# Two groups of stores on ScalarE's queue, an earlier bias strip, and two pinned silus in a two-layer kernel

## The chip, the cores and the metric

The kernel runs on one core of one Trainium2 chip, as one program. The metric is the device time of that program in microseconds, the median of several runs. Five engines work side by side, each through its own instructions in a fixed order: TensorE (PE; its weight loads are listed as PEld), VectorE (DVE), ScalarE (ACT), GpSimd (POOL) and SyncE (SP). An engine that meets an instruction whose inputs are not ready stands still, and so does all that is queued behind it. Transfers between the core's memory and DRAM are issued by an engine as an instruction and then run on 16 DMA engines.

## The reference, cut to what matters

Two blocks on x of 1024 positions by 1024 features, float32. The first is a gated delta rule beside a stick-breaking attention. The second is this:

```python
z = rms_norm(x) @ w_in
y_mla  = mla_group(z)     # q, k by two small projections, rms norm, rope; 8 heads, block-causal softmax
y_diff = diff_group(z)    # 4 heads, two maps each: softmax(q k + bias[bucket(k - q)]), a0 - lam * a1
x = x + concat(y_mla, y_diff) @ w_out
h = rms_norm(x)
g = causal_conv3(h @ w_gate) + conv_b
x = x + (silu(g) * (h @ w_up)) @ w_down
x = x + sigmoid(rms_norm(x) @ w_ple_gate) * (p @ w_ple_proj)
```

## The kernel before

A float32 factor is kept as a rounded high half and the remainder as a low half, and a product takes three matmuls (`mm3`: high by high, high by low, low by high). Weights come from DRAM as a `raw` tile and are split into an `hl` pair (`W`, with POOL doing both halves, L255 and L256). A scheduler puts the instructions of all engines in an order from priorities; code in a `high_priority` block is moved ahead of what was written before it, and `keep_in_program_order` holds an instruction behind all that its engine was given before. Every transfer of this kernel is issued by SP.

**Staged projections.** `qk_stack` (queries and keys of the stick-breaking attention in layer 1, of the diff attention in layer 2) and `mla_proj` (the latent attention) compute rows by position, normalize them, transpose them on PE (L768, L1151) into a PSUM tile, and split that tile into a staging tile: ACT casts the high half (L313), DVE subtracts for the low half (L314; both lines are in the helper `split_evac`). The staging tile goes to DRAM: 32 tiles `qb_st` from L771 (16 in each layer, into `dr_qk` and `dr_dqk`) and 32 tiles `l_st` from L1154 (into `dr_mla`, 384 KB each). There are three `l_st` buffers, and two `qb_st` buffers in layer 1 but one in layer 2. In the same stretch ACT squares the PSUM results (`qb_sq` L750, `l_sq` L1103 and L1125), DVE multiplies by gains, sums the squares and takes the inverse root (L291 to L306), and POOL scales by it.

**Start of the diff attention.** It comes after the latent attention, interleaved with `ple_proj` (the product of p with `w_pp`, whose results `p_o` go to DRAM as `dr_pp`, L1454 and L1455, two buffers). For each head, `first` loads a bias `strip` (512 KB, L1309), and POOL fills a corner of it (L1311). DVE then adds the strip to the logits `z` of a block and takes the row maximum (L1341, L1342), ACT takes the exponential (L1344), and PE transposes (L1364) and multiplies by the values (L1367). The weight `lam` of the second map is loaded at L1284 and worked out on DVE and ACT (L1286 to L1293). `ahead` runs before, within the latent attention, and loads the first head's queries and keys.

**The feed-forward product.** `ffn` has 11 groups of 256 hidden features. A group is two calls of `wino`, one for the gate and one for the up product, each seven products of 128x512 with twelve matmuls. The seven, in PE's order, are B11 into accumulator x, B21 into z, T2 onto x, T1 into y, T3 onto x, T4 into q and B22 onto y. Between them ACT copies x out three times (`w_u`, L1571; below u1, u2 and u3): T2 may not start before u1 is out, nor T3 before u2. `out` adds an accumulator and a copy: in the up product that is `f_c` (DVE, L1621), followed by `f_y` = `f_y` times `f_c` (DVE, L1622), for the four quarters (0,0) with u1, (1,1) with u3, (1,0) and (0,1). B22 may not start before `f_c` of (1,1) has read y. `f_y` holds the convolution of the gate product (DVE, L1612 and L1614), and the silu (ACT, L1616) is applied to it in place, in two halves: ct 1 first, then ct 0, the half that `f_y` of (0,0) needs.

Of the kernel before, what the change touches and what calls it, by code (L numbers as in the profile page):

```python
# [11 lines left out]
F32 = mybir.dt.float32  # L12
# [152 lines left out]
class Kern:  # L165
# [572 lines left out]
    def qk_stack(self, pool, xn, ws, gains, dst):  # L738
# [23 lines left out]
        def stack(gi, half, raw):  # L762
            for pr in range(2):
# [7 lines left out]
                nc.sync.dma_start(dst[p, :, a:a + 2, half * 512:half * 512 + 512], st.bitcast(F32))  # L771
# [277 lines left out]
    def mla_proj(self):  # L1049
# [96 lines left out]
        def fin(raw, hg, half, part):  # L1146

            for h in range(4):
                pt = self.PT()
                for j in range(4):  # L1150
                    nc.tensor.transpose(pt[:96, j, :], raw[:, j, h, :], self.ident)  # L1151
                st = lp.tile([96, 2, 512], F32R, tag="l_st", name="l_st", bufs=3)
                self.split_evac(st[:, 0], st[:, 1], pt[:96].rearrange("p a b -> p (a b)"))
                nc.sync.dma_start(self.dr_mla[4 * hg + h, 0:96, part:part + 2, half * 512:half * 512 + 512], st.bitcast(F32))  # L1154
# [110 lines left out]
    def ahead(self):  # L1265
# [4 lines left out]
        self.qk0 = self.load_qk(self.qp, self.dr_dqk[0], 0)  # L1270
        yield 0.0

    def diff(self):
# [30 lines left out]
        def first(hd):  # L1304
            qk = [self.load_qk(qp, self.dr_dqk[hd], 0) if hd else self.qk0]
            o = sp.tile([128, NT, 128], F32, tag="o", name="o", bufs=2)
            skew = self.dr_f[hd][0:1, 127:128]
            strip[hd] = sp.tile([128, 1024], F32, tag="strip", name="strip", bufs=2)
            nc.sync.dma_start(strip[hd], bass.AP(tensor=skew.tensor, offset=skew.offset, ap=[[1152, 128], [1, 1024]]))  # L1309

            nc.gpsimd.memset(strip[hd][0:64, 960:1024], NEG)  # L1311
# [125 lines left out]
    def ple_proj(self):  # L1437

        nc, d = self.nc, self.d
        with self.pool("pp") as fp:  # L1440
            pT = [self.pair(fp, f"pT{h}", 2) for h in range(2)]
            for h in range(2):
                for k in range(2):
                    pr = fp.tile([128, 512], F32, tag="p_raw", name="p_raw", bufs=1)
                    nc.sync.dma_start(pr, d["pT"][:, k, h * 512:h * 512 + 512])
                    nc.scalar.copy(pT[h][0][:, k], pr)
                    nc.gpsimd.tensor_tensor(pT[h][1][:, k], pr, pT[h][0][:, k].bitcast(F32), ALU.subtract)
            for gi in range(4):
                w = self.W(d["w_pp"][gi])
                for tp in range(4):  # L1450
                    ps = self.tm(w, pT, 2, tp)
                    for j in range(2):
                        o = fp.tile([128, 256], F32, tag="p_o", name="p_o", bufs=2)
                        nc.scalar.copy(o, ps[:, j])  # L1454
                        nc.sync.dma_start(self.dr_pp[gi, tp, :, j], o)  # L1455
                    yield 0.25
# [135 lines left out]
    def ffn(self):  # L1592

        nc, d, tc, vec = self.nc, self.d, self.tc, self.vec
        with self.pool("ffn", 1) as fp:
            for gi in range(11):
# [19 lines left out]
                silu = lambda y: nc.scalar.activation(y, y, AF.Silu)  # L1616
# [104 lines left out]
```

## Time and profile before

| what | value |
|---|---|
| time, median of 3 runs | 2645.79 us (2638.98 to 2645.89) |
| the profiled execution | 2637.64 us |
| its span, first to last instruction | 2635.9 us |
| mean granted TensorE clock | 0.982 |
| PE busy, share of the span | 2490.2 us, 94% |
| DVE, POOL, ACT busy | 1435.8, 1054.8, 869.3 us (54%, 40%, 33%) |
| DMA engines, mean | 119 GB/s |

Busy time is summed for each engine over the span; the engines overlap. A clock of 1.00 is TensorE's higher level, 2.4 GHz, and 0.50 its lower, 1.2 GHz. The profiled execution lies 1.3 us below the fastest of the three runs and 8.2 us below their median. PE has 146 us of the span in which it does nothing, spread over the stages.

### The profile page before, as it was taken

How to read it: one execution, taken by the hardware profiler on the slowest of the kernel's cores; microseconds unless marked ns; L12 is line 12 of the kernel's file. 1: busy time of each engine (PE TensorE's matmuls, PEld its weight loads, DVE VectorE, ACT ScalarE, POOL GpSimd, SP SyncE). 2: the span in 40 equal slices, each digit the busy share in tenths (PEclk: the TensorE clock that was granted, in tenths of full speed). 3: DMA queues.
4: the chain of work that ended last, by engine and by line, in shares of the span. 5: the costliest groups of instructions: out<-in, count | busy, mean ns of one | idle time of the engine just before them, and what ended most of it. 6: DMA issues, size and time to landing. Idle time of an engine off the chain costs nothing.

```text
span 2635.9 us, 38621 instructions
## 1 busy us (share of the span) xinstructions
PE 2490.2 (94%) x15170; PEld 2119.0 (80%) x15170; DVE 1435.8 (54%) x2677; ACT 869.3 (33%) x1599; POOL 1054.8 (40%) x914
## 2 busy tenths in 40 slices
PE   6999999999999999998899989988999999999999
PEld 6888999876777779988787868887777777777789
DVE  5565555275666553368854338846544544433372
ACT  3322223163444341123334346624333333100030
POOL 1524332122122245544533322224777777533322
PEclk9999999999999999999999999989999999999999
DMA  4433223253422455322675457451222122523222
GB/s 163 141 110 112 81 89 105 65 151 97 116 84 69 167 177 180 115 72 90 203 214 167 120 186 205 136 188 58 67 92 80 64 89 87 185 79 104 72 85 93
DMA packets 158766, 313.55 MB, mean 119 GB/s; under 512 B 14804, under 2 KB 62164, under 8 KB 158456
## 3 DMA queue, kind: packets, MB, share of 16 engines
q1 hardware_dynamic: 158584, 311.07, 37.8%
q8 instruction: 120, 1.97, 0.3%
q14 instruction: 62, 0.51, 0.1%
HBM read 214.01 MB, written 100.42 MB: 119 GB/s over the span
## 4 chain that ended last, share of the span: by engine, by line
PE 40%; DVE 9%; DMA 3%; issue 2%; ACT 2%; POOL 1%; SPq 0%; ACTq 0%; DVEq 0%; POOLq 0%
PE pj L1567 13%; PE pj L266 6%; PE pj L264 6%; PE pj L265 6%; DVE f_y L1614 1%; PE po L932 1%; PE pt L925 1%; PE po L1367 1%; DVE f_y L1612 1%; PE z L1337 1%; PE z L264 1%; DVE rs_a L304 1%; PE z L265 1%; PE z L266 1%; DMA f_y<-dr_h 1%
## 5 line engine op out<-in xcount | busy, mean ns | idle before, releaser
L255 POOL TENSOR_SCALAR hl<-raw 128x512 fp32r<-128x512 f32 (+2 forms) x262 | 192.7, 740 | 897.4 <-PE pj L266 884.1
L256 POOL TENSOR_TENSOR hl<-raw,hl 128x512 fp32r<-128x512 f32 (+3 forms) x270 | 367.7, 1369 | 34.0 <-ACT hl L253 17.9
L265 PE MATMUL pj<-hl,xn_0h 128*128 128x256 f32 (+2 forms) x544 | 159.0, 292 | 2.7 <-POOL hl L256 2.7
L264 PE MATMUL pj<-hl,xn_0h 128*128 128x256 f32 (+2 forms) x544 | 160.4, 295 | 0.6 <-DVE qb_st L314 0.6
L264 PE MATMUL pj<-hl,xn_1h 128*128 128x256 f32 (+2 forms) x544 | 159.6, 293 | 0.0
L266 PE MATMUL pj<-hl,xn_0l 128*128 128x256 f32 (+2 forms) x544 | 159.3, 293 | 0.0
L265 PE MATMUL pj<-hl,xn_1h 128*128 128x256 f32 (+2 forms) x544 | 157.3, 289 | 0.0
L266 PE MATMUL pj<-hl,xn_1l 128*128 128x256 f32 (+2 forms) x544 | 157.2, 289 | 0.0
L1548 POOL TENSOR_TENSOR hl<-w_s,hl 128x512 fp32r<-128x512 f32 x88 | 117.6, 1341 | 66.9 <-ACT hl L1547 66.7
L266 PE MATMUL pj<-hl,f_hl 128*128 128x512 f32 x352 | 139.8, 399 | 2.3 <-DVE f_hl L1653 2.3
L264 PE MATMUL pj<-hl,f_hh 128*128 128x512 f32 x352 | 139.7, 397 | 2.0 <-DVE xres L1662 1.6
L1548 POOL TENSOR_TENSOR hl<-raw,hl 128x512 fp32r<-128x512 f32 x66 | 103.1, 1568 | 91.5 <-ACT hl L1547 91.5
L265 PE MATMUL pj<-hl,f_hh 128*128 128x512 f32 x352 | 138.9, 395 | 0.0
L1662 DVE TENSOR_TENSOR xres<-xres,pj 128x512 f32<-128x512 f32 x96 | 65.2, 686 | 129.9 <-PE pj L266 118.2
L264 PE MATMUL pj<-xn_0h,hl 128*128 128x512 f32 x288 | 117.6, 408 | 0.0
L264 PE MATMUL pj<-xn_1h,hl 128*128 128x512 f32 x288 | 116.6, 405 | 0.0
L927 DVE COPY aT<-pt 128x512 f32<-128x512 f32 (+1 forms) x112 | 70.6, 630 | 83.6 <-PE pt L925 83.4
L265 PE MATMUL pj<-xn_1l,hl 128*128 128x512 f32 x288 | 116.1, 403 | 0.0
L266 PE MATMUL pj<-xn_0h,hl 128*128 128x512 f32 x288 | 115.1, 400 | 0.0
L265 PE MATMUL pj<-xn_0l,hl 128*128 128x512 f32 x288 | 114.8, 398 | 0.0
L266 PE MATMUL pj<-xn_1h,hl 128*128 128x512 f32 x288 | 114.4, 397 | 0.0
L1605 DVE TENSOR_TENSOR f_u<-pj,w_u 128x512 f32<-128x512 f32 x44 | 30.3, 689 | 148.6 <-ACT w_u L1571 96.5
(595 smaller groups left out, 7316.9 us busy)
## 6 DMA issues: line engine op xcount, KB each, us to landing
raw<-in_w_o_dram SPq DMA_DIRECT2D x28, 512.0 KB
qk<-dr_mla SPq DMA_DIRECT2D x32, 416.0 KB
dr_mla<-l_st SPq DMA_DIRECT2D x32, 384.0 KB
raw<-in_w_fg_dram SPq DMA_DIRECT2D x22, 512.0 KB
raw<-in_w_fu_dram SPq DMA_DIRECT2D x22, 512.0 KB
dr_h<-f_y SPq DMA_DIRECT2D x22, 512.0 KB
raw<-in_w_fd_dram SPq DMA_DIRECT2D x22, 512.0 KB
f_y<-dr_h SPq DMA_DIRECT2D x22, 512.0 KB
```

The costliest lines, as they stand in the source:

```text
L255: nc.gpsimd.tensor_scalar(hl[:, 0], raw[:, k:k + c], 1.0, 1.0, ALU.mult, ALU.mult)
L256: nc.gpsimd.tensor_tensor(hl[:, 1], raw[:, k:k + c], hl[:, 0].bitcast(F32), ALU.subtract)
L264: mm(ps, lh[0], rh[0], start=first, stop=False)
L265: mm(ps, lh[0], rh[1], start=False, stop=False)
L266: mm(ps, lh[1], rh[0], start=False, stop=last)
L304: nc.vector.tensor_tensor(a, y, y, ALU.mult)
L925: nc.tensor.transpose(pt[:, b, :], e[a][:, j * 128:j * 128 + 128], self.ident)
L927: copy[j0 // 2 % 2](aT[:, :n], pt[:, :n])
L1548: nc.gpsimd.tensor_tensor(hl[:, 1], v, hl[:, 0].bitcast(F32), ALU.subtract)
L1567: nc.tensor.matmul(ps, w[k][l], b[r][:, k, :], start=first and k + n == 0, stop=k == 3 and n == 2, skip_group_check=not first)
L1605: nc.vector.tensor_tensor(u, ps, v, ALU.add)
L1662: nc.vector.tensor_tensor(xr, xr, ps, ALU.add)
```

## The change

The stores of L771 and L1154 are issued by ACT in place of SP. The first strip is loaded in `ahead` by a new function, and the strips' tile moves from the diff attention's pool to the pool that `ahead` opens. `ple_proj` loads its four weights first and holds one pair of tiles `pT` at a time, one half of the positions after the other, where it held both. The two silus of a feed-forward group are kept in program order, behind the copies u2 and u3 of the up product. The line numbers of the changed kernel are 5 higher from L1310 on.

```diff
@@ qk_stack
-                nc.sync.dma_start(dst[p, :, a:a + 2, half * 512:half * 512 + 512], st.bitcast(F32))
+                nc.scalar.dma_start(dst[p, :, a:a + 2, half * 512:half * 512 + 512], st.bitcast(F32))
@@ mla_proj, fin
-                nc.sync.dma_start(self.dr_mla[4 * hg + h, 0:96, part:part + 2, half * 512:half * 512 + 512], st.bitcast(F32))
+                nc.scalar.dma_start(self.dr_mla[4 * hg + h, 0:96, part:part + 2, half * 512:half * 512 + 512], st.bitcast(F32))
@@ ahead
         self.qk0 = self.load_qk(self.qp, self.dr_dqk[0], 0)
+        self.strip0 = self.load_strip(0)
         yield 0.0
+
+    def load_strip(self, hd):
+        skew = self.dr_f[hd][0:1, 127:128]
+        strip = self.qp.tile([128, 1024], F32, tag="strip", name="strip", bufs=2)
+        self.nc.sync.dma_start(strip, bass.AP(tensor=skew.tensor, offset=skew.offset, ap=[[1152, 128], [1, 1024]]))
+
+        self.nc.gpsimd.memset(strip[0:64, 960:1024], NEG)
+        return strip
@@ diff, first
-            skew = self.dr_f[hd][0:1, 127:128]
-            strip[hd] = sp.tile([128, 1024], F32, tag="strip", name="strip", bufs=2)
-            nc.sync.dma_start(strip[hd], bass.AP(tensor=skew.tensor, offset=skew.offset, ap=[[1152, 128], [1, 1024]]))
-
-            nc.gpsimd.memset(strip[hd][0:64, 960:1024], NEG)
+            strip[hd] = self.load_strip(hd) if hd else self.strip0
@@ ple_proj
-            pT = [self.pair(fp, f"pT{h}", 2) for h in range(2)]
+            ws = [self.W(d["w_pp"][gi]) for gi in range(4)]
             for h in range(2):
+                pT = self.pair(fp, "pT", 2)
                 for k in range(2):
                     pr = fp.tile([128, 512], F32, tag="p_raw", name="p_raw", bufs=1)
                     nc.sync.dma_start(pr, d["pT"][:, k, h * 512:h * 512 + 512])
...
-            for gi in range(4):
-                w = self.W(d["w_pp"][gi])
-                for tp in range(4):
-                    ps = self.tm(w, pT, 2, tp)
...
+                for gi in range(4):
+                    for tp in range(2 * h, 2 * h + 2):
+                        ps = self.tm(ws[gi], [pT, pT], 2, tp)
...
@@ ffn
-                silu = lambda y: nc.scalar.activation(y, y, AF.Silu)
+                silu = lambda y: tc.keep_in_program_order(nc.scalar.activation(y, y, AF.Silu))
```

The scheduler turns this into new orders. The first place is ScalarE in the projections of layer 2, where the tiles `l_st_12000` to `l_st_12027` are staged (numbers tell the buffers apart). Before, SP holds their four stores behind two weight loads of the diff attention's value projection:

```order
L248 DMA raw_13798<-in_w2_dv_dram 128x1024 [waits DMAHW4_49,Pool_49]
L248 DMA raw_13806<-in_w2_dv_dram 128x1024 [waits DMAHW5_49,Pool_49]
L1154 DMA dr_mla_10149<-l_st_12000 96x2x512 [waits DMAHW6_49,DVE_49]
L1154 DMA dr_mla_10149<-l_st_12009 96x2x512 [waits DMAHW7_49,DVE_49]
L1154 DMA dr_mla_10149<-l_st_12018 96x2x512 [waits DMAHW0_49,DVE_49]
```

In the changed kernel the stores stand on ACT, each behind the cast of its high half and some of them behind or ahead of a square:

```order
L313 CAST l_st_12000<-pt_11995 96x512 [waits DMAHW7_49,PE_49]
L313 CAST l_st_12009<-pt_12004 96x512 [waits DMAHW1_49,PE_49]
L1154 DMA dr_mla_10149<-l_st_12000 96x2x512 [waits DVE_49]
L750 ACTIVATE qb_sq_11991<-pj_11942 128x512 [waits PE_49]
L1154 DMA dr_mla_10149<-l_st_12009 96x2x512 [waits DVE_49]
L313 CAST l_st_12018<-pt_12013 96x512 [waits DMAHW2_49,PE_49]
L313 CAST l_st_12027<-pt_12022 96x512 [waits DMAHW4_49,PE_49]
```

The weight loads are no longer ahead of the stores, and each store now waits on ACT for DVE's low half, with the next square or cast queued behind it.

The second place is ScalarE in the feed-forward product, one up product of the middle groups. Before:

```order
L1547 CAST hl_18738<-raw_18734 128x512 [waits DMAHW3_49,PE_49,Activation_49]
L1616 ACTIVATE f_y_18579<-f_y_18579 128x1024 [waits DMAHW4_49,DVE_49]
L1547 CAST hl_18741<-raw_18736 128x512 [waits DMAHW5_49,PE_49,Activation_49]
L1571 COPY w_u1_18635<-pj_18620 128x512
L1616 ACTIVATE f_y_18583<-f_y_18583 128x1024 [waits DMAHW6_49,DVE_49]
```

In the changed kernel:

```order
L1552 CAST hl_18741<-raw_18736 128x512 [waits DMAHW5_49,PE_49,Activation_49]
L1576 COPY w_u1_18635<-pj_18620 128x512 [waits DVE_49]
L1552 CAST hl_18748<-w_s_18746 128x512 [waits PE_49,Activation_49,Pool_49]
L1552 CAST hl_18751<-w_s_18744 128x512 [waits PE_49,Activation_49]
L1576 COPY w_u2_18661<-pj_18620 128x512 [waits DVE_49]
L1621 ACTIVATE f_y_18579<-f_y_18579 128x1024 [waits DMAHW4_49,DVE_49]
L1552 CAST hl_18756<-w_s_18754 128x512 [waits PE_49,Activation_49,Pool_49]
L1552 CAST hl_18759<-raw_18736 128x512 [waits PE_49,Activation_49]
L1576 COPY w_u3_18688<-pj_18620 128x512
L1621 ACTIVATE f_y_18583<-f_y_18583 128x1024 [waits DMAHW6_49,DVE_49]
```

The copy u1 has lost the silu ahead of it, and the silu that `f_y` of (0,0) needs (`f_y_18583`) stands behind u3. DVE's order of `f_c` and `f_y` is as before: (0,0), then (1,1). The third place is TensorE at the end of such an up product, where B22 follows T4. In the changed kernel four matmuls of the next gate product stand between them; before, B22 followed T4 directly and B11 came after it:

```order
L1572 MATMUL pj_18411<-T4h_17985,hl_18326 128x512
L1572 MATMUL pj_18481<-B11h_17389,hl_18452 128x512
L1572 MATMUL pj_18481<-B11l_17390,hl_18452 128x512
L1572 MATMUL pj_18481<-B11h_17389,hl_18452 128x512 x2
L1572 MATMUL pj_18336<-B22h_17983,hl_18331 128x512
```

So B22 starts four matmuls later in PE's row. The last group has no gate product behind it and keeps the old order there.

## Rows read from the trace of the kernel before

**Rows 1.** Busy time by stretch: PE, PEld, DVE, ACT, POOL, clock, DMA share

```profile
1230.00:1250.00 20.00, 16.25 (x105) 15.58 (x104) 20.00 (x43) 6.26 (x13) 12.39 (x10) 0.85 0.43 135
1308.00:1330.00 22.00, 21.95 (x171) 21.64 (x170) 19.23 (x68) 7.82 (x18) 8.56 (x6) 0.90 0.78 246
...
1577.00:1586.00 9.00, 7.76 (x26) 6.33 (x27) 6.19 (x32) 5.41 (x19) 0.00 (x0) 0.53 0.70 264
...
1853.00:1894.00 41.00, 40.23 (x167) 32.42 (x167) 16.88 (x20) 12.95 (x22) 30.59 (x22) 0.96 0.21 70
```

**Rows 2.** Timelines of DVE, SP, ACT and PE around 1300 (start, us, engine, line)

```profile
1293.31 1.87 DVE L314 TENSOR_TENSOR l_st<-pt,l_st 96x512 fp32r<-96x512 f32 x3
...
1297.06 4.03 SPq L248 DMA_DIRECT2D raw<-in_w_dv_dram  x2
1301.18 2.86 SPq L1154 DMA_DIRECT2D dr_mla<-l_st  x3
...
1306.27 0.58 ACT L313 CAST l_st<-pt 96x512 fp32r<-96x512 f32 x1 [7.92 <-DMA dr_mla<-l_st]
...
1307.62 1.09 PE L1151 MATMUL pt<-cst,l_raw 128*96 128x128 f32 x4 [7.45 <-DVE l_st L314]
```

**Rows 3.** Instructions of the staging tile's store (ns: least, median, most)

```profile
L1154 SPq DMA_DIRECT2D dr_mla<-l_st x32: 304/327/1890, 1234.3 to 1338.1; - x32
```

**Rows 4.** Timelines of ACT and DVE: both halves of one staging tile

```profile
1243.56 0.58 ACT L313 CAST l_st<-pt 96x512 fp32r<-96x512 f32 x1 [0.23 <-PE pt L1151]
...
1248.84 0.68 DVE L314 TENSOR_TENSOR l_st<-pt,l_st 96x512 fp32r<-96x512 f32 x1
...
1290.97 0.60 ACT L750 ACTIVATE qb_sq<-pj 128x512 f32<-128x512 f32 x1 [5.78 <-DVE rs_y L306]
```

**Rows 5.** Timelines of SP, ACT, POOL and PE at the diff attention's start

```profile
1569.50 0.35 SPq L1284 DMA_DIRECT2D lam<-in_lam_dram  x1
...
1570.96 0.32 SPq L1309 DMA_DIRECT2D strip<-dr_f  x1
...
1569.90 0.37 ACT L1454 COPY p_o<-pj 128x256 f32<-128x256 f32 x1 [2.98 <-DMA dr_pp<-p_o]
...
1573.92 0.29 DVE L1286 TENSOR_TENSOR lam_p<-lam 128x128 f32<-128x128 f32 x1 [6.48 <-DMA lam<-in_lam_dram]
...
1576.43 0.14 POOL L1311 MEMSET strip<- 64x64 f32 x1 [7.90 <-DMA strip<-dr_f]
...
1576.96 0.47 PE L1337 MATMUL z<-k,q 128*128 128x128 f32 x1 [9.91 <-DVE a_nm L1341]
```

**Rows 6.** PE's waits from 1813 to 2270: total, times, longest

```profile
PE pj L1567 <- ACT w_u L1571: 10.4, 10, 2.0
```

**Rows 7.** Timelines of PE in the first group, of ACT in the second

```profile
1853.77 0.51 PE L1567 MATMUL pj<-T2h,hl 128*128 128x512 f32 x1 [2.02 <-ACT w_u L1571]
...
1893.21 1.06 ACT L1616 ACTIVATE f_y<-f_y 128x1024 f32<-128x1024 f32 x1 [3.72 <-DVE f_y L1614]
```

**Rows 8.** Timelines of PE, ACT, DVE and POOL around T4 of the second group

```profile
1903.75 0.39 PE L1567 MATMUL pj<-T4h,hl 128*128 128x512 f32 x1
...
1906.53 0.40 PE L1567 MATMUL pj<-B22h,hl 128*128 128x512 f32 x1
...
1904.53 0.58 ACT L1571 COPY w_u<-pj 128x512 f32<-128x512 f32 x1
...
1898.59 0.69 DVE L1622 TENSOR_TENSOR f_y<-f_y,f_c 128x512 f32<-128x512 f32 x1 [0.32 <-ACT f_y L1616]
1905.14 0.69 DVE L1621 TENSOR_TENSOR f_c<-pj,w_u 128x512 f32<-128x512 f32 x1 [5.86 <-ACT w_u L1571]
1905.87 1.72 DVE L1622 TENSOR_TENSOR f_y<-f_y,f_c 128x512 f32<-128x512 f32 x1
...
1905.76 1.28 POOL L1553 TENSOR_TENSOR w_s<-w_s,raw 128x512 f32<-128x512 f32 x1
```

**Rows 9.** Timeline of PE at the end of the last group

```profile
2270.19 0.50 PE L1567 MATMUL pj<-B22h,hl 128*128 128x512 f32 x1 [3.28 <-DVE f_c L1621]
```

More of the change, by code (lines that the diff above doesn't have):

```diff
@@ L1445, in ple_proj @@
                     nc.sync.dma_start(pr, d["pT"][:, k, h * 512:h * 512 + 512])
-                    nc.scalar.copy(pT[h][0][:, k], pr)
-                    nc.gpsimd.tensor_tensor(pT[h][1][:, k], pr, pT[h][0][:, k].bitcast(F32), ALU.subtract)
-            for gi in range(4):
-                w = self.W(d["w_pp"][gi])
-                for tp in range(4):
-                    ps = self.tm(w, pT, 2, tp)
[L1452 to L1456, printed above, removed]
+                    nc.scalar.copy(pT[0][:, k], pr)
+                    nc.gpsimd.tensor_tensor(pT[1][:, k], pr, pT[0][:, k].bitcast(F32), ALU.subtract)
+                for gi in range(4):
+                    for tp in range(2 * h, 2 * h + 2):
+                        ps = self.tm(ws[gi], [pT, pT], 2, tp)
+                        for j in range(2):
+                            o = fp.tile([128, 256], F32, tag="p_o", name="p_o", bufs=2)
+                            nc.scalar.copy(o, ps[:, j])
+                            nc.sync.dma_start(self.dr_pp[gi, tp, :, j], o)
+                        yield 0.25
     def mix_late(self):
```

## The prediction

> **What bounds the kernel now.** I read the page first. PE is busy for 2490 of 2636 us, and the change takes no matmul away, so a gain can only come from the 146 us in which PE stands still and from the time in which its clock is at the lower level. I then listed PE's idle stretches with what ended each, and looked at the four places that the change touches.
>
> In the projections of layer 2, PE stands still once for 7.45 us [rows 2]. The chain behind it: the transposes L1151 waited for DVE's low half, that for ACT's cast, and the cast had waited 7.92 us for a staging buffer, which three stores still held. DVE had finished the three low halves at 1293.31 + 1.87 = 1295.2, but SP issued the stores only from 1301.18, because two weight loads stood ahead of them from 1297.06 to 1301.09. So the data were ready 6 us before the stores went. In the 22 us after the stretch the clock is 0.90 [rows 1]: 22 x 0.10 = 2.2 us more. Elsewhere in this stage DVE is full: all 20.00 of 20 us, with PE at 16.25 [rows 1].
>
> At the diff attention's start PE stands still for 9.91 us [rows 5]. The strip was issued at 1570.96 and its corner filled at 1576.43, 5.4 us later; the first maximum and PE's next matmul follow. Then the clock is 0.53 for 9 us [rows 1], its lower level nearly throughout: 9 x 0.47 = 4.2 us.
>
> In the feed-forward product PE waits ten times for a copy `w_u`, 10.4 us [rows 6]: 2.02 us in the first group [rows 7], (10.4 - 2.02) / 9 = 0.93 in nine others. It is u1, held up by a silu of 1.06 us [rows 7] that waits for the convolution. After the first one the clock is 0.96 over 41 us [rows 1], 1.6 us. The last group has another wait, 3.28 us, before B22 [rows 9].
>
> **The stores on ACT.** Taken away: the 7.45 us, with the 2.2 us of clock, 9.7 at most, since the stores would go at 1295.2, while ACT casts its next `l_st` only after 1300. Added: an issue takes 0.33 us (median) [rows 3], and the 48 of layer 2 come to 16 us of an engine that is a third busy. That is cover enough, but for the order. A store waits on ACT for DVE's low half, which can be late: one tile's cast ended at 1244.1 and its low half at 1249.5, 5.4 us after [rows 4]. Squares queue behind the store, DVE sums them, and DVE is full here, so what it waits for is not made good. I price one such hand-over by the square and the issue, 0.60 + 0.33 = 0.9 us [rows 3, 4]. Where the next instruction of DVE does not need that square, it costs nothing. I take 6 hand-overs of the 48, 5.7 us, since the full stretches are only part of the stage and PE is not always behind DVE: 9.7 - 5.7 = **-4 us**. Bounds: -10 with none, +8 with 20 of them. In layer 1 the 16 stores are covered by the same free ACT; 0, bound +5 (16 x 0.33, every issue paid).
>
> A page of the Trainium skill speaks against this part: DMA: Bandwidth & Descriptors, "Issuing engines are not separate DMA queues", says that transfers from all engines run on the same 16 DMA engines and that a second issuing engine saves only the issue time. By that alone this part would bring 0. The row shows another loss than bandwidth, a store behind a waiting load in one engine's order, so I keep -4 and carry the rule as a rival.
>
> **The strip and `ple_proj`.** Taken away: 9.91 + 4.2 = 14.1 us. Late next are three things. `lam` took 1573.92 - 1569.50 = 4.4 us to arrive [rows 5] and its place in the row is hardly earlier; but the first maxima no longer stand behind it, and matmuls of `ple_proj` now lie between the first logits and the transposes. The `p_o` copies wait for their stores, up to 2.98 us [rows 5], and now share ACT with the diff attention's exponentials. And the second pair `pT` can be filled only when the first half's last matmul is done: cast 0.58, subtraction 1.28 (like POOL's in [rows 8]), a load of half the strip's size (estimate 2.7 to 5.4 us from its 5.4), again cast and subtraction, 6.4 to 9.1 us; matmuls of the latent attention cover perhaps 5 of it. I charge 2.5 for the pair and 4.5 for the other two: 14.1 - 7 = **-7 us**. Bounds: -13 with nearly all hidden, 0 when what is late next takes the whole place of the strip.
>
> **The silus.** u1 comes free, so the ten waits go. In their place B22 waits. Before, u3 ended at 1904.53 + 0.58 = 1905.1. Now the silu follows, to 1906.1; then DVE does `f_y` of (0,0), and only after it `f_c` of (1,1), 0.69 us, which B22 needs. `f_y` takes 0.69 us alone but 1.72 us where a POOL operation of 1.28 us has just begun [rows 8]. So y is read at 1906.1 + 0.69 + 0.69 = 1907.5, or at 1908.5. B22 stood at 1906.53 and now has four matmuls more ahead of it, (1906.53 - 1903.75) / 12 = 0.23 each [rows 8]: due at 1907.46. The new wait is about 0.1 or 1.1 us. POOL is busy for 30.6 of 41 us here [rows 1], so I take 0.8.
>
> The rule for this is on the page SBUF — State Buffer, "Who interferes with whom": a DVE instruction with two inputs in SBUF contends with a GpSimd instruction that reads SBUF, and the loser waits for the whole instruction. The trace agrees (1.72 against 0.69); were it so every time, this part would cost 9 x (1.1 - 0.93) = +1.5 in the middle groups, and by the short row it would bring -7.5.
>
> Middle groups: 9 x (0.8 - 0.93) = -1.2. First group: 2.02 + 1.6 goes, 0.8 comes: -2.8. Last group: no gate product follows, and `f_c` of (1,1) stands behind one more `f_y`: +1.0 (0.69 to 1.72). Together **-3 us**, bounds -10 and +1.
>
> **Sum.** 2637.64 - 4 - 7 - 3 = 2623.6. The profiled execution lies 1.3 us below the fastest of the three runs and 8.2 below their median, so the median may come out higher than the sum; I forecast 2625. 0.3% (8 us) is about what a measurement of this kernel can tell from no change.
>
> **Rivals.**
> 1. All three waits go and nothing comes back: -10 - 13 - 10 gives 2605; two of three about 2612. For it: the data stood ready 6 us before the stores, and nothing but the strip held DVE at 1576. Against it: DVE is full in the one stage, and the second `pT` has a chain of its own. Chance 0.17.
> 2. What is late next takes the place: the strip's 14 us go to the second `pT` and the `p_o` stores, and the silus to B22. 2637.64 - 4 + 0 + 1 = 2635. For it: ACT already waits for `p_o` stores. Chance 0.17. The case of the first page's rule, the stores bring 0 and the rest is as forecast, gives 2628; chance 0.08, and lies within the forecast's range.
> 3. The feed-forward wait is moved and PE's clock falls after it, as after the 2.02 us: 10 x 1.6 = 16 us on top of the forecast, 2641. Against it: after the nine waits of 0.93 us the middle groups keep their pace; for it: the new wait may reach 1.1 and more. Chance 0.08.
> 4. Slower: ACT, held by stores that wait for DVE, holds DVE in turn. If all 48 hand-overs are paid, 48 x 0.9 = 43 us against 9.7: 2637.64 + 33 - 10 = 2661. It decides from 31 hand-overs on (31 x 0.9 = 28, the 9.7 + 7 + 3 of the gains and 8 us more). For it: DVE is full and low halves come up to 5.4 us late. Against it: ACT is a third busy and works ahead. Chance 0.08.
>
> **How the numbers follow.** The forecast has 0.42; its own range is 2615 to 2635, from the three terms' bounds taken one at a time. The first rival reaches down to 2605 and the second and third up to 2641; 2608 to 2644 leaves out some 2 in 10. Faster by over 0.3%, below 2637.9 against the median shown: nearly all of the forecast and rival 1, the page's case, and about half of rival 2, which after the 8 us between profile and median lies at the edge: 0.66. Slower: rival 4 and a little of 3: 0.09. The rest, 0.25, is the same.
>
> **What would show it.** Right: no idle stretch of PE above 2 us at 1300 and no cast waiting 7.92 us for a store; the first maximum at once after the latent attention's last matmul; `w_u` gone from PE's waits, and `f_c` L1626 there about ten times at 0.1 to 1.1 us. Wrong: ACT waiting long at its stores while DVE idles before L752 or L1105; PE waiting for `pTl` or for `p_o` copies; a clock below 0.95 in the middle groups. The forecast fails most easily at the 6 hand-overs, which no row counts, and at the 7 us charged at the diff attention's start.

## Result and the profile after

The changed kernel takes 2626.43 us (median of 4 runs, 2625.82 to 2628.09), the kernel before 2644.97 (4 runs, 2638.98 to 2645.89). The ratio is 0.9936, with a 95% interval from 0.9921 to 0.9952: faster by 0.6%, more than the 0.3% that a measurement can tell from no change. The profiled execution takes 2626.64 us, 11.0 less than that of before; the medians differ by 18.5, because the profile of before lay below its runs.

The page of the changed kernel, its span and its busy times:

```profile
span 2624.8 us, 38588 instructions
...
PE 2488.8 (95%) x15170; PEld 2118.0 (81%) x15170; DVE 1435.2 (55%) x2677; ACT 866.9 (33%) x1599; POOL 1074.6 (41%) x914
```

PE does the same work in 11 us less span. Where they came from is read from PE's rows that open a stage: the first transpose `pt<-cst,n_xs` of layer 2, the first transpose of the latent projections (L1091), the first logits `z` of the latent attention, the last matmul on a `mix` tile, the first feed-forward product. The differences of their start times, in us:

| stage | before | changed | difference | predicted |
|---|---|---|---|---|
| layer 1 | 1071.3 | 1068.9 | -2.4 | 0 |
| projections, from L1091 to the latent attention | 155.4 | 161.9 | **+6.5** | -4 |
| latent and diff attention, to the last `mix` matmul | 450.2 | 442.6 | **-7.6** | -7 |
| feed-forward product to the end | 807.1 | 799.7 | **-7.4** | -3 |

The row that parts the second line of this table from the third, the first logits of the latent attention, does not stand at the same place in PE's work. Of the 480 matmuls `pj<-hl,xn_0h` and `pj<-hl,xn_0l` between L1091 and the last `mix` matmul, 359 stand ahead of it before and 384 in the changed kernel. They follow each other at 0.12 us, so 25 x 0.12 = 3.0 us of the +6.5, and as much of the -7.6, are work that moved from one line to the other. At equal work the two lines read +3.5 and -4.6; their sum is not touched.

**Projections.** The 7.45 us in which PE stood still [rows 2] are gone from their place, and the stage is longer. The whole stage, before and in the changed kernel (PE, PEld, DVE, ACT, POOL, clock, DMA share):

```profile
1194.30:1349.66 155.36, 134.51 (x986) 128.45 (x983) 128.15 (x340) 52.09 (x111) 74.71 (x60) 0.95 0.56 176
```

```profile
1191.60:1353.46 161.86, 140.92 (x1011) 134.10 (x1009) 124.82 (x340) 51.75 (x111) 74.81 (x60) 0.94 0.55 169
```

PE does nothing for 155.36 - 134.51 = 20.85 us before and for 161.86 - 140.92 = 20.94 now: the idle time of the stage did not fall at all. Of the +6.5, 3.0 are the moved matmuls and some 1.6 the clock (0.94 in place of 0.95); the rest is not put down to anything here. PE's waits now (line, what was waited for, total, times, longest):

```profile
PE pt L1151 <- POOL l_raw L1110: 5.4, 2, 3.2
PE pt L1151 <- DVE l_st L314: 4.8, 3, 3.0
PE pt L768 <- DVE l_st L314: 3.4, 1, 3.4
PE pt L768 <- POOL qb_raw L759: 2.4, 1, 2.4
PE pt L1151 <- DVE qb_st L314: 2.1, 1, 2.1
```

One long gap has become several shorter ones, most of them waits for a scaled row of POOL or a low half of DVE. In the busiest 50 us DVE is no longer full. Before, and in the changed kernel:

```profile
1250.00:1300.00 50.00, 47.30 (x331) 43.63 (x330) 46.86 (x130) 20.17 (x49) 25.63 (x21) 0.96 0.62 199
```

```profile
1250.00:1300.00 50.00, 43.15 (x291) 39.37 (x290) 40.55 (x117) 18.78 (x46) 24.49 (x18) 0.91 0.68 215
```

(The stage starts 2.7 us earlier in the changed kernel. Counted from its first row, DVE is busy for 47.8 and 42.8 us between 54 and 104.) What can hold DVE stands on ACT. ACT's timeline shows two stores (`ACTq`) and the cast behind them:

```profile
1241.41 0.49 ACT L1103 ACTIVATE l_sq<-pj 128x384 f32<-128x384 f32 x1 [0.56 <-PE pj L266]
1245.47 0.38 ACTq L771 DMA_DIRECT2D dr_dqk<-qb_st  x1
1246.63 0.31 ACTq L1154 DMA_DIRECT2D dr_mla<-l_st  x1
1247.04 0.58 ACT L313 CAST l_st<-pt 96x512 fp32r<-96x512 f32 x1 [5.13 <-DVE l_st L314]
```

The square ended at 1241.90 and ACT then did nothing for 5.13 us, because two stores stood in its row, each until DVE had written its low half. In all of layer 2 (1180 to 1430) ACT stands before 33 of the 48 stores, from the end of its instruction before to the issue, for 37.1 us together. Not all of this is loss, since some of that time ACT would have waited for something else. ACT's and POOL's waits in the stage sum up what follows:

```profile
ACT l_st L313 <- DVE l_st L314: 5.7, 2, 5.1
...
POOL l_raw L1110 <- DVE rs_y L306: 20.0, 3, 10.3
POOL l_raw L1131 <- DVE rs_y L306: 18.4, 4, 12.0
...
POOL l_raw L1110 <- DVE rs_a L304: 3.2, 1, 3.2
```

and before:

```profile
ACT l_st L313 <- DVE l_st L314: 0.8, 1, 0.8
```

```profile
POOL l_raw L1131 <- DVE rs_y L306: 12.7, 3, 5.5
POOL l_raw L1131 <- DVE rs_a L304: 8.9, 1, 8.9
...
POOL l_raw L1110 <- DVE rs_y L306: 8.9, 2, 5.0
```

So POOL waits longer for the inverse roots, 41.6 us in place of 30.5, and PE for the rows that POOL scales, 7.8 (5.4 and 2.4) in place of 3.7.

**Diff attention.** The strip is loaded at 1510.2 and its corner filled at 1522.0, within the latent attention. The first maximum, DVE's row at the start, and what PE and ACT waited for next:

```profile
1572.78 0.28 DVE L1346 CUSTOM_DVE_ANT_0 e<-z,strip 128x128 f32<-128x128 f32 x1
...
1576.87 0.39 PE L264 MATMUL pj<-hl,pTh 128*128 128x256 f32 x1 [2.59 <-ACT p_o L1459]
...
1575.37 0.37 ACT L1459 COPY p_o<-pj 128x256 f32<-128x256 f32 x1 [3.81 <-DMA dr_pp<-p_o]
...
1580.06 0.29 DVE L1295 TENSOR_TENSOR lam_p<-lam 128x128 f32<-128x128 f32 x1 [2.16 <-DMA lam<-in_lam_dram]
```

The 9.91 us [rows 5] are gone. What is late next is the pair of the prediction: the `p_o` stores (3.81 us for ACT, 2.59 for PE) and `lam` (2.16 for DVE). The second pair `pT` cost PE one wait of 0.30 us. The clock there is 0.76 over 14 us, 14 x 0.24 = 3.4 us; before it was 0.53 over 9 us [rows 1], 4.2 us. So the idle time is gone, and most of what the clock cost is still there.

```profile
1576.00:1590.00 14.00, 11.53 (x63) 10.12 (x63) 10.11 (x40) 9.56 (x32) 2.07 (x3) 0.76 0.72 216
```

**Feed-forward product.** The ten waits for `w_u` [rows 6] are gone, and one row of PE's waits stands in their place:

```profile
PE pj L1572 <- DVE f_c L1626: 9.3, 5, 4.7
```

It has 5 waits and not about ten: 1.15 to 1.18 us in the first group and three middle groups, 4.69 in the last, and none of 0.6 or more in the other six. A middle group with the wait, its row of PE and of DVE and POOL at that place:

```profile
1940.70 0.50 PE L1572 MATMUL pj<-B22h,hl 128*128 128x512 f32 x1 [1.17 <-DVE f_c L1626]
...
1938.01 1.84 DVE L1627 TENSOR_TENSOR f_y<-f_y,f_c 128x512 f32<-128x512 f32 x1 [5.68 <-ACT f_y L1621]
...
1938.02 1.29 POOL L1553 TENSOR_TENSOR hl<-raw,hl 128x512 fp32r<-128x512 f32 x1
```

and the same two instructions in the group before, which has no wait:

```profile
1898.74 0.69 DVE L1627 TENSOR_TENSOR f_y<-f_y,f_c 128x512 f32<-128x512 f32 x1 [5.61 <-ACT f_y L1621]
...
1898.81 1.79 POOL L1553 TENSOR_TENSOR hl<-raw,hl 128x512 fp32r<-128x512 f32 x1
```

In the first, the two begin within 0.01 us of each other and `f_y` takes 1.84 us. In the second, `f_y` begins 0.07 us ahead and takes 0.69, POOL takes 1.79 in place of 1.29, and PE waits for nothing. The first ten groups all meet like this: `f_y` took 0.69 us in the six in which it began 0.01 to 0.07 us ahead of POOL, and 1.82 to 1.84 in the four in which POOL began between 0.03 us ahead of it and 0.01 behind.

### The profile page after: what moved, and what is told of

It reads as the page before. It is cut to its first block, busy times and chain, and to the rows that moved or that the text cites. A ratio compares the mean times of both kernels' runs of the same rounds, so it can differ in the third digit from the quotient of the medians.

```text
span 2624.8 us, 38588 instructions
## 1 busy us (share of the span) xinstructions
PE 2488.8 (95%) x15170; PEld 2118.0 (81%) x15170; DVE 1435.2 (55%) x2677; ACT 866.9 (33%) x1599; POOL 1074.6 (41%) x914
## 4 chain that ended last, share of the span: by engine, by line
PE 41%; DVE 7%; DMA 4%; ACT 2%; issue 2%; POOL 1%; SPq 0%; ACTq 0%; DVEq 0%; POOLq 0%
PE pj L1572 16%; PE pj L266 6%; PE pj L264 6%; PE pj L265 6%; PE po L932 1%; PE pt L925 1%; PE po L1372 1%; DMA f_y<-dr_h 1%; DMA qk<-dr_mla 1%; DVE e L1346 1%; DMA dr_dqk<-qb_st 1%; DVE rs_a L304 1%; DVE rs_a L305 1%; DMA dr_dv<-vt 0%; PE z L264 0%
## 5 line engine op out<-in xcount | busy, mean ns | idle before, releaser
L265 PE MATMUL pj<-hl,xn_1h 128*128 128x256 f32 (+2 forms) x544 | 157.6, 290 | 0.0
L1553 POOL TENSOR_TENSOR hl<-w_s,hl 128x512 fp32r<-128x512 f32 x88 | 130.0, 1477 | 56.7 <-ACT hl L1552 56.1
L1553 POOL TENSOR_TENSOR hl<-raw,hl 128x512 fp32r<-128x512 f32 x66 | 111.7, 1692 | 71.3 <-ACT hl L1552 70.4
L265 PEld LDWEIGHTS pj<-hl,xn_0h 128*128 128x128 f32 x544 | 104.4, 192 | 4.6 <-POOL hl L256 3.6
```

Of the source, the lines that this page charges most:

```text
L265: mm(ps, lh[0], rh[1], start=False, stop=False)
L1553: nc.gpsimd.tensor_tensor(hl[:, 1], v, hl[:, 0].bitcast(F32), ALU.subtract)
```

## The experiments

Two theories stood against each other. **Hold**: the stores themselves are well placed early, but a store that waits on ACT for DVE's low half holds ACT's row, and this costs more than the 7.45 us that it saves. **Scatter**: the order that the scheduler makes of any change shifts this stage by several us, and the stores are not the cause. The stage times of all runs, measured as in the table above (us):

```
                      layer 1  projections  to mix   ffn to end
before                 1071.3     155.4      450.2     807.1
e1_silu_only           1069.7     155.1      453.4     800.1
e10_ple_only           1072.4     155.5      455.5     807.6
e4_act_only            1069.2     160.9      450.1     807.6
changed                1068.9     161.9      442.6     799.7
e11_changed_again      1068.8     159.8      437.0     800.7
e2_mla_on_sp           1073.4     157.6      450.0     801.8
e3_all_on_sp           1074.4     154.8      442.4     800.7
e6_late_store          1076.4     161.6      446.9     799.7
e7_shared_3            1074.1     154.7      438.4     800.6
e8_shared_4            1074.4     154.8      439.2     801.2
e9_split_store         1075.4     148.7      442.6     800.9
e5_silus_at_u2         1073.2     154.8      441.5     790.5
e12_u2_again           1074.1     153.9      446.9     790.2
```

e1 to e4 ran on one chip (kernel before there: 2639.65 us, median of 23 runs), e5 to e12 on another, in two batches (2639.52, 13 runs, beside e5 to e8; 2638.72, 17 runs, beside e9 to e12). Each ratio is to the kernel before in the same batch.

The moved work has to be taken out of the column of the projections. Ahead of its last row stand 359 of the 480 matmuls in the kernels with all stores on SP (355 in e8_shared_4), 384 in changed, e11_changed_again and e4_act_only, 351 in e2_mla_on_sp, 355 in e6_late_store and 323 in e9_split_store. And the last row itself waits, for `qk` or for its issue, by 0.39 to 5.70 us. At 0.12 us for a matmul, the projections are, at equal work (359 everywhere), and without that last wait:

```
                                  equal work      without the last wait
all stores on SP (eight kernels)  153.9 to 155.5  152.2 to 153.4
changed, and run again            158.9, 156.8    157.3, 155.7
e4_act_only                       157.9           157.2
e6_late_store                     162.1           156.9
e2_mla_on_sp                      158.6           152.9
e9_split_store                    153.1           152.7
```

In the last column the four runs in which unsplit stores of L1154 stand on ACT (changed, changed again, e4_act_only, e6_late_store) lie 2.3 us or more above all the others.

**e1_silu_only**: the kernel before, with the two silus pinned and nothing else.

```diff
-                silu = lambda y: nc.scalar.activation(y, y, AF.Silu)
+                silu = lambda y: tc.keep_in_program_order(nc.scalar.activation(y, y, AF.Silu))
```

> The kernel before with only the two silus kept in program order. Theory (each part acts in its own stage, as the two traces read against each other say): the feed-forward product and what follows it lose 7.3 us, nothing else moves; about 2630 us for a profiled run of 2637.6, ratio 0.9972. B22 waits for f_c in 3 to 5 of the 11 groups, 1.2 us each, and u1 in none. Rival (part of those 7.3 us comes from the rest of the change, by a luckier meeting of f_y with GpSimd): 2633 to 2637 us, ratio 0.998 to 1.000, with B22 waiting in most groups.

2634.75 us, ratio 0.9985 (0.9972 to 0.9997). The feed-forward stage fell by 7.0 us, as in the changed kernel (7.4), and B22 waits in five groups, so this gain belongs to the silus alone. The whole gained only 4.9 us, which is the rival's number and not its cause: in the profile the attentions, which this edit does not touch, took 3.2 us more.

**e4_act_only**: the kernel before, with both stores on ACT and nothing else (the same edit at L771 and L1154).

```diff
-                nc.sync.dma_start(
+                nc.scalar.dma_start(
```

> The kernel before with only the stores moved to ScalarE. Theory: layer 1 wins 2.4 us, layer 2's projections lose 8.7: 6 us slower than before, about 2644 for a profiled run of 2637.6, ratio 1.002; TensorE idle for over 25 us between 1170 and 1400, with ScalarE's casts waiting behind stores. Rival (the forecast's term, a gain of 4 us, with the loss due to something else in the change): 2634 us, ratio 0.998.

2643.26 us, ratio 1.002 (1.0003 to 1.0037). The whole is 3.6 us longer, and the projections grew by 5.5 us (2.5 at equal work, 4.0 without the last wait), as in the changed kernel (6.5, 3.5 and 4.1): this part alone loses. PE's idle time from 1170 to 1400 was expected above 25 us; it is 23.5, against 24.5 before, so the loss does not lie in that.

**e3_all_on_sp**: the changed kernel, with both stores back on SP.

```diff
-                nc.scalar.dma_start(
+                nc.sync.dma_start(
```

> The changed kernel with all staged stores back on SyncE: the strip, ple_proj and the silus alone. Theory: layer 1 gives back its 2.4 us, the projections of layer 2 win 8.7 us: 2626.4 + 2.4 - 8.7 = 2620 us, ratio 0.991, and the idle stretch of 7.4 us at 1300 is there again. Rival (the strip's gain of 10 us was in part a catching up of what the projections had lost): 2625 to 2630 us, ratio 0.993 to 0.995.

2622.83 us, ratio 0.9937 (0.9917 to 0.9957). The gap came back, 7.41 us, and yet the projections are 7.1 us shorter than in the changed kernel (4.1 at equal work). The other gains stay; here, where no work moved, the strip and `ple_proj` bring 7.8 us (442.4 against 450.2). The ratio is nevertheless that of the changed kernel, since layer 1 is 5.5 us longer here (below).

**e2_mla_on_sp**: the changed kernel, with only the stores of L1154 back on SP; those of L771 stay on ACT.

```diff
-                nc.scalar.dma_start(self.dr_mla[4 * hg + h, 0:96, part:part + 2, half * 512:half * 512 + 512], st.bitcast(F32))
+                nc.sync.dma_start(self.dr_mla[4 * hg + h, 0:96, part:part + 2, half * 512:half * 512 + 512], st.bitcast(F32))
```

> The changed kernel with the latent attention's stores (dr_mla<-l_st) back on SyncE; the q and k stores stay on ScalarE. Theory (in layer 2 the stores held ScalarE until VectorE's low half was there, and this costs 8.7 us between 1170 and 1380): most of it is given back, 6 us less, about 2620 us, ratio to before 0.991. Rival (the stage lost its time to the new order that the scheduler made, not to the stores): within 2 us of the changed kernel, 2625 to 2628 us, ratio 0.993 to 0.994.

2631.71 us, ratio 0.997 (0.9957 to 0.9982), slower than either expectation. The projections take 157.6 us, but 5.70 of it are a wait for `qk` at its last row. Without that wait and at equal work it has 152.9, like the kernels with all stores on SP: the loss is that of the L1154 stores. The L771 stores alone cost nothing there, although ACT stands before them for 17.6 us. The strip's gain is missing in this run (450.0, as before) although the strip is early. Why this stage kept its old length stays open.

**e5_silus_at_u2**: e3_all_on_sp, with both silus behind the copy u2, so that the one which `f_y` of (0,0) needs no longer follows u3.

```diff
-                          {"u2": lambda: silu(ys[1]), "u3": lambda: silu(ys[0])})
+                          {"u2": lambda: [silu(ys[1]), silu(ys[0])]})
```

> All stores on SyncE, strip and ple_proj as changed, and both silus kept behind the copy u2 (the changed kernel has one behind u2 and one behind u3). Theory (what is left of the feed-forward waits is f_c of (1,1) behind f_y, which waits for the silu behind u3): B22 waits in no group but the last, the product ends about 5 us earlier than with one silu at each copy: ratio 0.992 to before, 5 us below the kernel with all stores on SyncE. Rival (the casts that now stand behind two silus are late, and TensorE waits for a weight's halves instead): no faster than that kernel, with waits on L1553 or L1552 in the middle groups.

2612.32 us, ratio 0.9906 (0.9882 to 0.993). The feed-forward stage fell by another 10.2 us against e3_all_on_sp. PE's waits there hold one wait for `f_c`, in the last group:

```profile
PE pj L1572 <- DVE f_c L1626: 2.6, 1, 2.6
```

So B22's wait was made by the silu behind u3, and no wait of the rival's kind came. The gain is twice the 5 us expected. This version beats both kernels. **e12_u2_again** is the same kernel in the later batch:

> The kernel with all stores on SyncE and both silus behind u2 once more, beside the changed kernel on one chip. Theory: 10 to 14 us below the changed kernel, ratio 0.989 to 0.991 to before; the feed-forward product 10 us shorter than in the changed kernel. Rival (half of its lead was scatter): 5 to 8 us below the changed kernel.

2616.44 us, ratio 0.9921 (0.9902 to 0.994), with the same stage at 790.2; 9.9 us below the changed kernel in the same batch (e11_changed_again).

**e6_late_store**: the changed kernel, with each store of L1154 issued one tile later on ACT, when its low half should be ready.

```diff
+        late = []
...
-                nc.scalar.dma_start(self.dr_mla[...], st.bitcast(F32))
+                late.append((self.dr_mla[...], st.bitcast(F32)))
+                if h:
+                    nc.scalar.dma_start(*late.pop(0))
+            nc.scalar.dma_start(*late.pop(0))
```

> The changed kernel with each dr_mla store issued on ScalarE one tile later, behind the next tile's cast, so that the low half has more time. Theory (ScalarE is held by stores whose low half is not there): the stretch from the first l_st to the last gives back about half of the 5 us that it lost, the run is 2 to 4 us below the changed kernel, ratio 0.992. Rival (the loss is not in the hold: the stage is bound by VectorE and by the order): within 1.5 us of the changed kernel, ratio 0.9935.

2635.58 us, ratio 0.9984 (0.9969 to 1.0). The projections did not fall (161.6; 156.9 in the last column, as in the changed kernel), which by what was expected speaks for Scatter. The edit did not do what it was meant to, though: stores stand together on ACT behind one low half, and ACT stands before stores for 43.4 us in place of 37.1. The whole is 9 us longer than the changed kernel, of which 7.5 lie in layer 1.

**e7_shared_3** and **e8_shared_4**: e3_all_on_sp with the rotation's scratch in the ring of the squares (the control), and the same with a fourth `l_st` buffer, so that the cast need not wait for a store on SP.

```diff
-            s = lp.tile([128, 4, 4, 32], F32, tag="l_s", name="l_s", bufs=1)[:, :, :n]
+            s = squares().rearrange("p (t h f) -> p t h f", t=4, h=4)[:, :, :n]
...
-                st = lp.tile([96, 2, 512], F32R, tag="l_st", name="l_st", bufs=3)
+                st = lp.tile([96, 2, 512], F32R, tag="l_st", name="l_st", bufs=4)
```

> Control for the next run: all stores on SyncE, strip, ple_proj and silus as changed, and the rotation's scratch tile taken from the ring of the squares (room for one more staging buffer). Expected by every theory: within 3 us of the kernel with all stores on SyncE, ratio about 0.994; the idle stretch of 7.4 us before L1151 at about 1305 is there.

> The control with four l_st buffers in place of three: a store that SyncE issues late no longer holds the next cast, and ScalarE issues nothing. Theory (the idle stretch at 1300 is worth its 7.4 us and the clock after it, and on ScalarE the hold ate it): the stretch goes and the projections of layer 2 end 6 to 9 us earlier than in the control, ratio about 0.991. Rival (the stretch is slack: behind it the stage is bound by the chain of transposes, splits and roots, so removing it moves the wait): the stretch goes, smaller waits come, and the projections end within 2 us of the control.

2618.7 us (0.9925, 0.9903 to 0.9948) and 2620.91 (0.9928, 0.9901 to 0.9955). The expected 6 to 9 us did not come. The gap shrank only from 7.46 to 6.0 us, so the run doesn't tell what the whole gap is worth; the 1.5 us of it moved nothing, 154.7 against 154.8.

**e9_split_store**: the changed kernel, with each store in two: the high half from ACT, whose cast has just written it, and the low half from SP. No store on ACT waits for DVE any more.

```diff
-                nc.scalar.dma_start(self.dr_mla[4 * hg + h, 0:96, part:part + 2, half * 512:half * 512 + 512], st.bitcast(F32))
+                for n, q in enumerate((nc.scalar, nc.sync)):
+                    q.dma_start(self.dr_mla[4 * hg + h, 0:96, part + n, half * 512:half * 512 + 512], st[:, n].bitcast(F32))
```

(the same at L771)

> The changed kernel with every staged store in two: the high half on ScalarE, which wrote it and so waits for no other engine, the low half on SyncE. ScalarE issues as many stores as in the changed kernel. Theory (in layer 2 ScalarE is held by stores that wait for VectorE's low half; squares and with them the roots come late): the hold is gone, the stretch from the first to the last matmul of the projections gives back 4 to 6 us, GpSimd's longest wait for a root falls from 12 to about 9 us, the run is near the kernel with all stores on SyncE: ratio 0.991 to 0.992, beside the changed kernel's in this call. Rival (issuing on ScalarE or the scheduler's new order costs it, not the wait): no less than 1.5 us below the changed kernel.

2620.3 us, ratio 0.9934 (0.9919 to 0.9949), and the projections take 148.7 us: 13.2 less than in the changed kernel and 6.1 less than with all stores on SP. But 61 and 36 matmuls fewer stand in them; at equal work and without the last wait, 152.7, they are 4.6 shorter than in the changed kernel, 3.0 shorter than in its second run, and as long as with all stores on SP (152.7 in e3_all_on_sp). ACT's row now reads

```profile
1247.02 0.58 ACT L313 CAST l_st<-pt 96x512 fp32r<-96x512 f32 x1 [0.47 <-PE pt L1152]
1247.63 0.31 ACTq L1156 DMA_DIRECT2D dr_mla<-l_st  x1
1248.05 0.49 ACT L1104 ACTIVATE l_sq<-pj 128x384 f32<-128x384 f32 x1 [0.44 <-DVE rs_i L301]
```

cast, store and square close behind each other. ACT stands before its stores for 6.4 us in all, in place of 37.1. In the 50 us from 1250 DVE is full again (40.55 us in the changed kernel; between 54 and 104 us from the stage's first row 47.0 against 42.8):

```profile
1250.00:1300.00 50.00, 44.14 (x309) 41.15 (x310) 47.10 (x128) 17.71 (x41) 27.06 (x22) 0.93 0.64 210
```

This speaks for Hold: there are as many stores on ACT and more issues in all, and the loss goes once they wait for nothing but ACT's own cast. Scatter fits badly: the orders of e2_mla_on_sp, e6_late_store and e9_split_store all differ, and yet the last column falls into two groups by one thing alone, whether unsplit stores of L1154 stand on ACT. What stays open is the size of the loss, since one program differs by 1.6 us between two runs in this column: 2.5 to 4.1 us above the kernel before. And the split gains nothing over stores on SP: the whole, 2620.3 us, is that of e7_shared_3 and e8_shared_4 (2618.7 and 2620.91), although it is 6.0 below the changed kernel in the same batch. POOL's longest wait for a root fell from 12.0 to 10.1 us, not to 9, and its waits for roots still sum to 35.1. Split stores together with e5_silus_at_u2 were not run.

**e10_ple_only**: the kernel before, with the new `ple_proj` and nothing else. (The early strip without the new `ple_proj` was not run.)

```diff
-            pT = [self.pair(fp, f"pT{h}", 2) for h in range(2)]
+            ws = [self.W(d["w_pp"][gi]) for gi in range(4)]
             for h in range(2):
+                pT = self.pair(fp, "pT", 2)
...
```

> The kernel before with only ple_proj in its new form (four weights first, one pair pT); the strip is loaded where it was. Theory (the strip is what held the diff attention, ple_proj only makes room): the first maximum waits for the strip again, 6 to 10 us of TensorE idle; about as before or up to 3 us slower for the second pT, ratio 1.000 to 1.001. Rival (a good part of the gain is the new order of ple_proj, whose last matmuls now lie in the diff attention's start): 3 to 6 us faster, ratio 0.998.

2642.89 us, ratio 1.0012 (1.0 to 1.0024). The stage to the last `mix` matmul is 455.5, 5.3 us longer, and the wait for the strip remains. One program differs by up to 5.6 us in this stage (442.6 and 437.0 for the changed kernel), so the 5.3 are no certain loss; but the new order of `ple_proj` brings nothing by itself. PE's wait at the first maximum is 9.65 us here, as expected.

**e11_changed_again**: the changed kernel once more, in the batch of e9_split_store.

> The changed kernel once more, beside the others on one chip, for the scatter between executions of one program. Theory: ratio 0.9936 within 0.002, the last matmul before layer 2 within 3 us of where it was, the projections of layer 2 again 5 to 6 us longer than with the stores on SyncE. Rival (that loss was scatter): less than 2 us longer.

2626.34 us, ratio 0.9956 (0.9942 to 0.997): a gain of 12.4 us, where the first runs had 18.5 and the two profiles 11.0. The projections are 159.8 us, 11.1 above e9_split_store and 5.9 above e12_u2_again; at equal work and without the last wait 3.0 and 3.5. Its eight runs spread from 2618.93 to 2631.29, and the profiled one is the fastest.

## Why the prediction was right, and where it was not

The prediction said 2625 us, 2608 to 2644, faster with 0.66; the time was 2626.43. Three of its terms must be told apart, since two errors offset each other, and that the total came so near is luck: against the profile the sum was -14.0, and the measured difference -11.0.

**The stores on ACT: -4 predicted, +6.5 measured (+3.5 at equal work). This step failed, with its sign.** The mechanism was named: "Squares queue behind the store, DVE sums them, and DVE is full here". What failed first is the price, 6 hand-overs at 0.9 us, 5.7 in the sum (6 x 0.93 is 5.6): ACT stood before 33 stores, for 37.1 us. One hand-over was taken as the square's and the issue's own time, and the low half's lateness was left out of it: a store that waits holds ACT as long as DVE is late, and one stretch with two such stores took 5.13 us. The trace of before had the number: over its 32 `l_st` tiles the low half ended 0.7 to 5.7 us after the high one, 1.9 in the mean; the 5.4 of [rows 4] is near the long end. The credit was wrong too. The 9.7 us of the gap and its clock were counted as time to be had, but PE's idle time in the stage is 20.9 us before and now, and its clock is not higher: other waits took the gap's place. The bound of +8 held it. In the chain from ACT's hold to POOL's late roots the ends are shown (5.13 us, and 41.6 us of POOL's waits in place of 30.5); that the squares carry it from one to the other is argued, and e9_split_store, without the hold, still has 35.1. For layer 1 the term of 0 is not contradicted: its length follows no store (below).

The page of the Trainium skill that the prediction weighed, DMA: Bandwidth & Descriptors, "Issuing engines are not separate DMA queues", gives 0 for such a move, the saved issue time apart. The runs differ where the store waits on the new engine for another's output: e4_act_only, the move alone, is 3.6 us longer as a whole, and 2.5 in the stage at equal work. Where each half goes from an engine that has it (e9_split_store), the stage is as long as with all stores on SP (152.7, and 152.2 to 153.4), and the page's 0 agrees.

**The strip and `ple_proj`: -7 predicted, -7.6 measured.** Right in mechanism, and the late-next things are those named: `p_o` and `lam`. Of the second pair's 2.5 us, 0.30 came. Of the 4.2 us of clock counted as taken away, 3.4 are still there. e10_ple_only shows that the new `ple_proj` alone doesn't bring the gain. The size is not firm: 3.0 of the 7.6 are work that moved out of the stage, e3_all_on_sp has 7.8 with none moved, the changed kernel gave 437.0 when run again, and e2_mla_on_sp and e12_u2_again 450.0 and 446.9 with the same early strip.

**The silus: -3 predicted, -7.4 measured.** Right in mechanism, wrong in size. The new wait of B22 was priced at 0.1 or 1.1 us, and so it came. The value chosen, 0.8 for a mean, was too near the long end: with three waits of 1.16 us in nine groups the mean is 3.5 / 9 = 0.39. The middle groups then bring 3.5 - 8.4 = -4.9 (predicted -1.2); the first, 1.18 - 2.02 - 1.6 = -2.4 (-2.8); the last, 4.69 - 3.28 = +1.4 (+1.0). A wait of 1.6 us after the last B22 is gone as well, which no step spoke of. The page of the Trainium skill that the prediction used, SBUF — State Buffer, "Who interferes with whom", has the one that issues first hold the shared port for its whole instruction, and the other wait. The trace agrees for `f_y` (1.84 us beside a POOL instruction of 1.29, 0.69 where it began clearly first). Six groups of nine don't lose, so the +1.5 that the prediction gave for a loss in every group did not come.

**The rivals.** The first (all gains, 2605) fails at the projections. Of the second, B22 takes part of the place of `w_u`, and the strip's does not come. The third needed a clock below 0.95 after the new waits; from 1884 to 2250 the clock is 1.00. The fourth (ACT holds DVE) is the one whose mechanism ran, at a size below the point from which it decides: e4_act_only has it alone, at +3.6 us in the whole. By the table's lines, that the whole came out near the forecast owes to the silus' 4.4 us more and layer 1's 2.4, against the stores' 10.5.

## What to carry to other kernels

Before a store is moved to the engine that writes one half of its data, look at who writes the other half: the engine then stands still until the later one is done, and how late that is is the price, not the issue. Leave such a store where it was, or split it so that each half goes from the engine that has it, or from one with nothing behind it; here the split took the loss away and gained nothing more. Where a gap is to be removed from a stage in which another engine is full, count as gain only what that engine can then do earlier. And before stage times are compared, count the instructions between the two marks: here 25 matmuls moved across one, and made up nearly half of a stage's difference.

## What the runs showed that was not expected

**Who comes first by a few hundredths of a us.** In the group without a wait DVE's `f_y` began 0.07 us ahead of POOL's subtraction and took 0.69 us; in the one with a wait the two began 0.01 us apart, and `f_y` took 1.84. Six of nine middle groups went without, one of them with a lead of only 0.01 us. Such a wait has no price between its ends; only the number of groups that fall on either side can be forecast.

**Layer 1 moves by 7.5 us with nothing changed in it.** In the changed kernel and in e6_late_store the order of all five engines is the same through all of layer 1, and layer 1 takes 1068.9 and 1076.4 us; the same program again took 1068.8. The windows from 930 to 950, of the changed kernel and then of e6_late_store:

```profile
930.00:940.00 10.00, 8.49 (x36) 6.33 (x35) 4.73 (x7) 5.41 (x9) 1.90 (x2) 1.00 0.87 294
940.00:950.00 10.00, 10.00 (x45) 8.06 (x44) 6.67 (x11) 5.80 (x9) 4.34 (x5) 1.00 0.37 109
```

```profile
930.00:940.00 10.00, 7.34 (x28) 5.32 (x28) 4.84 (x7) 4.08 (x7) 1.60 (x1) 0.90 0.79 247
940.00:950.00 10.00, 8.70 (x24) 6.13 (x23) 6.05 (x10) 5.86 (x9) 0.00 (x0) 0.59 0.53 181
```

PE waits for ACT's cast `oT11h` there, once for 1.28 us in the changed kernel, with the clock at its higher level throughout, and for 2.66 and 1.30 us in the other, with 0.90 and then 0.59:

```profile
936.96 0.49 PE L264 MATMUL pj<-oT11h,hl 128*128 128x512 f32 x1 [1.28 <-ACT oT11h L951]
```

```profile
938.70 0.79 PE L264 MATMUL pj<-oT11h,hl 128*128 128x512 f32 x1 [2.66 <-ACT oT11h L951]
941.94 0.80 PE L264 MATMUL pj<-oT11h,hl 128*128 128x512 f32 x1 [1.30 <-ACT oT11h L951]
```

PE's idle time in the two windows, 2.66 + 1.30 - 1.51 = 2.4 us more, and the clock, 10 x 0.10 + 10 x 0.41 = 5.1 us, make 7.5 us, the whole difference of the two. Why the casts came later there with the same order is open, and not all kernels follow it: e11_changed_again has 0.83 at 930 and still 1068.8. For this program a difference of a few us between two kernels is read by stages, not from the whole time.
